# Tying weight sums and transposes behind products, and gating one conv quarter earlier, in a one-core hybrid decoder layer

## The chip, the cores and the metric

The kernel runs on one core of one Trainium2 chip. The time of a run is the device time of that core in microseconds (us); the lower the better. The kernel before was run three times: 2455.8, 2457.36 and 2458.04 us, median 2457.36. One more execution was taken with the hardware profiler on; every duration below comes from it.

The engines of the core are named as the profile names them: PE (TensorE, matrix products), PEld (its weight loads, which overlap the products), DVE (VectorE, elementwise), ACT (ScalarE, activations and copies), POOL (GpSimd, which here issues DMAs and does little else) and SP (SyncE, which issues the weight loads). Each engine takes its instructions in the order of its own queue and waits at the head of it.

## The reference

One layer, 512 tokens, model width 2048, float32 throughout. Cut to what matters here:

```python
h = rmsnorm(x, g_mix)
z = h @ w_in                                  # conv B, C, V | Q, K, V | forget logits | two gates
conv_y = cb * causal_dwconv(cc * cv, conv_w)
conv_branch = conv_y @ w_conv_out             # 1024 -> 2048
attn = forgetting_attention(q, k, v, log_f)
attn_branch = attn @ w_attn_out               # 1024 -> 2048
merged = sigmoid(gate_c + b_c) * conv_branch + sigmoid(gate_a + b_a) * attn_branch
x = x + merged @ w_mix_out                    # 2048 -> 2048
h = rmsnorm(x, g_mlp)
u = square(relu(h @ w_ff1))                   # 2048 -> 8192
x = x + u @ w_ff2
return rmsnorm(x, g_final)
```

## The kernel before

**Products.** Most of the large products are done as seven products of half-size blocks instead of eight (a Strassen-Winograd scheme). The names are those of the scheme: A11 and A12 first (a group's head), then S1, S3, S2, S4 and A22 (its tail; the last mix group takes S1, S2, S4, S3, A22). The moving or stationary activations have seven forms of the same names, made by sums of their four quarters; the weights X[i, j] are summed on DVE while the group runs. Every float32 operand is split into a high part (rounded to fp32r, ACT) and a low part (the rest, DVE), and each block is multiplied three times: high by high, high by low, low by high. `Group.run` (L207) does this for one product: `split` writes a tile th and a tile tl (two buffers each), PE multiplies, and then the hook `self.after[name]` is called, which is where other work is placed between products. One product of 256 columns is 48 matmuls in the mix and the MLP's first product, and 24 in the conv output product, whose contraction is half as long.

**A group's order.** `head` (L241) loads X[0,0] and X[1,0], runs A11 and A12 and puts the first quarter of the output (0,0). `tail2` (L305) loads X[0,1] and X[1,1]; its *first sum* is X[0,1] - X[0,0], which S1 needs, its *third sum* X[1,1] - X[0,1], which S3 needs. It puts (1,1) after S2, (0,1) after S4 and (1,0) after A22. `first_sum` (L298) is a form of the first sum that is called from a hook: it loads X[0,1], and pins the sum. A pin (`tc.keep_in_program_order`) tells the planner, which otherwise orders each engine's queue by its own model of when inputs are ready, that an instruction may not be placed ahead of the one written just before it on the same engine. It says nothing about what may come in between, and adds no wait. Once a group is pinned, its third sum is pinned as well. In the kernel before only mix group 0 calls `first_sum`.

**The stages around the change**, each in four column quarters c or groups g of 512 columns:

- conv output products (`conv_out`, L918), in the order conv_out(0), attn_out(0), conv_out(1), (2), (3). Quarter 0 is multiplied by its gate where it is made; the others are stored to the DRAM tile held_d without a gate and brought back later (`bring`).
- attention output products (`attn_out`, L966), (1), (2), (3). `cons_at` takes one of the four 128-row results j: for c > 0 it loads the conv gate (hg), multiplies the conv branch by it (`onto`, L941), loads the attention gate (gt), multiplies the result by that and adds. A quarter's finished branch is then split into the seven operand parts M (`Products`, L869; `quads`, L885). The parts of quarter 3 go to two tiles, t2 and t3, which held the attention's operands: t3 those of the first chunk of the contraction, t2 those of the second. The parts of quarters 0 to 2 are made earlier. Those of quarter 3 are made from within the last attention product (A11, A12) and from the hooks of mix group 0.
- mix groups 0 to 3 (`Mix`, L1043, and the loop at L1133). `Mix.put` adds the residual (a load xr) to an output quarter, sums its squares, stores it and appends its transposition to `waiting`. `turn_waiting` (L1119) empties that list at chosen hooks: four PE transposes (ptr, L1075) for a quarter, two ACT copies with the gain into the tiles F (L1084), and for the quarter (0,1) two stores f_d of F's first half. `Mix.sums` forms the next operand's sums in place in F, and `out` splits and stores them (h_d). In group 3 `begin_part` loads the stored parts back into tiles that the mix no longer reads, as the operands of the MLP, and `fourth` loads the residual of the quarter (1,0).
- the first MLP group g0 (L1232), whose hooks finish the parts of group 3.

The pool `main` has a ring of five buffers with the tag "o", which the evacuated outputs, hg, gt, xr and the operand sums share. POOL issues the loads and stores of all these intermediate tiles from one queue; SP issues the loads of the weights and gt.

Of the kernel before, what the change touches and what calls it, by code (L numbers as in the profile page):

```python
# [45 lines left out]
def tile_hybrid_block(ctx: ExitStack, tc, x, g_mix, w_in, b_f, b_gate, conv_w, w_conv_out,  # L46
# [137 lines left out]
    class Group:  # L184
# [3 lines left out]
        def __init__(self, view, c1, c2, w, ST, mm, banks, put, scale=1.0, extra={}, after={}, shift=SHIFT):  # L188
            self.extra, self.after, self.shift = extra, after, shift
            self.view, self.cs, self.w, self.ST, self.mm, self.banks = view, (c1, c2), w, ST, mm, banks  # L190
            self.put, self.scale, self.at = put, scale, {}
            self.pinned = False
            self.nq = view.shape[0] // (2 * P)
# [722 lines left out]
    merged, quads3 = {}, {}  # L916

    def conv_out(c, banks):  # L918

        gates = {}  # L920
        if c == 0:
            for i, j in ((0, 0), (1, 1), (0, 1), (1, 0)):
                gates[i, j] = pc_.tile([P, 2, HS], F32, tag="hg", name="gates", bufs=4)
                k = 4 * c + 2 * j
                nc.gpsimd.dma_start(out=gates[i, j],
                                    in_=g_d[0, k:k + 2, :, i * HS:(i + 1) * HS].rearrange("k p s -> p k s"))
            place_merged(c)

        def put(i, j, v):
            ts = slice(i * HS, (i + 1) * HS)  # L930
            if c == 0:
                nc.vector.tensor_tensor(out=whole_of[c][:, i, :, j, :], in0=v, in1=gates[i, j], op=ALU.mult)
            else:
                nc.gpsimd.dma_start(out=held_d[c, 2 * j:2 * j + 2, :, ts].rearrange("k p s -> p k s"), in_=v)

        whole(Columns(w_conv_out, c * S, c * S + HS, HS, YS.get, mm_cols, tuple((b,) for b in banks), put,
                      extra={"A11": "first", "S3": "first"}))
# [28 lines left out]
    def attn_out(c, banks, last=False, **how):  # L966

        def cons_at(j, ps):
            if c > 0:
                hg = otile([P, S], "hg")  # L970
                nc.gpsimd.dma_start(out=hg, in_=g_d[0, 4 * c + j])
                onto(c, j, hg, ALU.mult)
# [4 lines left out]
            if last and j == 2:  # L977
                M.place(2, [(n, 3) for n in ("A11", "A12", "S1", "S2")])
                M.place(3, [("S4", 3), ("S3", 3), ("A22", 3), ("A22", 2)])
                for e in range(2):  # L980
                    nc.gpsimd.dma_start(out=M.at["A22", 2][e].bitcast(F32), in_=m22[e].bitcast(F32))
                quads3.update(M.quads(3, merged[3]))
                quads3["A11"]()
# [59 lines left out]
    class Mix:  # L1043
# [25 lines left out]
        def turn(self, i, j, v):  # L1069
# [3 lines left out]
            for par in range(2):  # L1073
                for t in range(2):
                    nc.tensor.transpose(pt[:, par, t * P:(t + 1) * P], v[:, t, par * P:(par + 1) * P], ident)  # L1075
# [46 lines left out]

    class Steps(dict):
# [9 lines left out]
    for g in range(4):  # L1133
        mix = Mix(g)
        after = Steps()
        if g == 0:
            for n, n2 in zip(("A12", "S1", "S3", "S2", "S4"), ("S1", "S3", "S2", "S4", "A22")):
                after.add(n, quads3[n2])
        if g == 3:
            after.add("S1", lambda: begin_part("A12", 4))  # L1140
        for n in ("A11", "S1", "A22") if g < 3 else ("A11", "S1", "S3"):
            after.add(n, turn_waiting)
        if before:
# [5 lines left out]
        else:  # L1149
            after.add("A12", lambda: begin_part("A11", 0))  # L1150
            after.add("S2", lambda: begin_part("S1", 1), lambda: begin_part("S3", 2))
            after.add("S4", mix.fourth, lambda: split_part("A11"))
            after.add("S3", lambda: begin_part("S2", 5))
            after.add("A22", lambda: begin_part("S4", 6), lambda: begin_part("A22", 3), lambda: split_part("A12"))
# [78 lines left out]
    g0.after = Steps(A11=[turn_waiting, mix.sums], A12=[lambda: mix.out("S1", mix.parts["S1"]),  # L1233
# [251 lines left out]
```

## Time and profile before

| | us |
|---|---|
| median of three runs | 2457.36 |
| the runs | 2455.8 to 2458.04 |
| the profiled execution, its own time | 2464.36 |
| its span, first to last instruction | 2462.6 |
| PE idle in the span (2462.6 - 2408.8) | 53.8 |
| conv_out(2) and (3), mix groups 0 to 3 and the first two products of the MLP | about 924 to 1239, with the attention products at 967 to 1033 |

How to read the views: a row of instructions gives the source line, the engine, the operation, the tiles written and read, the shape and the count; in the view in order of time it begins with its start and its duration, and the bracket at its end is how long the engine was idle ahead of it and what ended that. In a view of groups, the numbers behind the bar are the busy time, the mean duration in ns and the idle time ahead of them. A row of waits gives who waited for whom, the total in us, how often, and the longest. L104 is the low part of every split, L103 the high part, L113 every subtraction and L116 every addition. Matmuls are pipelined, so each lasts longer than the distance to the next one.

### The profile page before, as it was taken

Reading aid. Unit: us, or ns where it says so; the run is one execution under the profiler, and the core shown is the slowest. Engines: PE = TensorE matmul, PEld = TensorE weight load, DVE = VectorE, ACT = ScalarE, POOL = GpSimd, SP = SyncE. Lnnn points to the kernel's source line nnn. Section 1 sums busy time; section 2 is a strip of 40 time slices with the busy share of each in tenths; the row PEclk is TensorE's granted clock in tenths of the full one; section 3 lists DMA queues with packets and bytes.
Section 4 is the critical chain, followed back from the end, with each engine's and each line's share of the span. In section 5 each row is a group of like instructions: output and inputs, shape, how many; then the busy total and the mean of one; then the engine's idle time right before and its main releaser. Section 6 shows DMA issues by size and latency. Waiting matters only on the chain.

```text
span 2462.6 us, 41554 instructions
## 1 busy us (share of the span) xinstructions
PE 2408.8 (98%) x17800; PEld 2264.8 (92%) x17800; DVE 2041.8 (83%) x1729; ACT 1201.8 (49%) x1233; POOL 279.8 (11%) x450
## 2 busy tenths in 40 slices
PE   8999999999999999899899999999999999999998
PEld 8999899999999998799899999999997888888886
DVE  7987777788887777878888898888988888889898
ACT  6433443445555534355566666656655333333334
POOL 0100000111111112112200000000011000100000
PEclk9999999999999999999999999999999999999999
DMA  7664544454655746647855646556487576655662
GB/s 249 186 191 145 157 130 136 137 180 153 206 186 194 246 154 216 205 127 232 289 196 204 236 171 225 208 204 231 174 302 270 178 256 216 244 183 184 249 221 104
DMA packets 286588, 490.92 MB, mean 199 GB/s; under 512 B 11884, under 2 KB 198372, under 8 KB 286020
## 3 DMA queue, kind: packets, MB, share of 16 engines
q1 hardware_dynamic: 236032, 282.15, 36.0%
q0 software_dynamic: 49504, 205.02, 22.4%
q8 instruction: 139, 2.28, 0.4%
q10 hardware_dynamic: 868, 1.10, 0.1%
q14 instruction: 45, 0.37, 0.0%
HBM read 377.60 MB, written 110.10 MB: 198 GB/s over the span
## 4 chain that ended last, share of the span: by engine, by line
PE 48%; DVE 4%; DMA 3%; issue 2%; ACT 1%; POOL 0%; DVEq 0%; POOLq 0%; ACTq 0%
PE a L175 5%; PE a L173 5%; PE a L172 5%; PE a L153 3%; PE a L155 3%; PE a L157 3%; PE d L175 2%; PE d L153 2%; PE d L155 2%; PE d L172 2%; PE d L173 2%; PE d L157 2%; DVE tl L104 2%; PE c L153 1%; PE c L155 1%
## 5 line engine op out<-in xcount | busy, mean ns | idle before, releaser
L104 DVE TENSOR_TENSOR tl<-x,th 128x2048 fp32r<-128x2048 f32 (+1 forms) x280 | 639.1, 2288 | 177.0 <-ACT th L103 162.0
L103 ACT ACTIVATE th<-x 128x2048 fp32r<-128x2048 f32 (+1 forms) x280 | 536.9, 1918 | 498.6 <-DVE x L113 161.3
L113 DVE TENSOR_TENSOR x<-x,x 128x2048 f32<-128x2048 f32 (+1 forms) x160 | 365.9, 2287 | 29.8 <-DMA x<-in_w_in_dram 16.0
L103 ACT ACTIVATE th<-y 128x2048 fp32r<-128x2048 f32 (+1 forms) x109 | 185.0, 1701 | 276.0 <-PE a L173 138.8
L104 DVE TENSOR_TENSOR tl<-y,th 128x2048 fp32r<-128x2048 f32 (+1 forms) x109 | 219.0, 2013 | 26.0 <-ACT th L103 25.5
L172 PE MATMUL a<-th,us 128*128 128x512 f32 x512 | 199.4, 389 | 1.8 <-ACT th L103 1.8
L173 PE MATMUL a<-th,us 128*128 128x512 f32 x512 | 199.2, 389 | 0.0
L153 PE MATMUL c<-S,th 128*128 128x256 f32 x848 | 196.5, 277 | 0.0
L155 PE MATMUL c<-S,th 128*128 128x256 f32 x848 | 196.0, 277 | 0.0
L153 PE MATMUL a<-S,th 128*128 128x256 f32 x784 | 182.2, 278 | 0.0
L155 PE MATMUL a<-S,th 128*128 128x256 f32 x784 | 180.8, 276 | 0.0
L153 PEld LDWEIGHTS c<-S,th 128*128 128x128 f32 x848 | 159.3, 188 | 0.3
L155 PEld LDWEIGHTS c<-S,th 128*128 128x128 f32 x848 | 159.3, 188 | 0.0
L155 PEld LDWEIGHTS a<-S,th 128*128 128x128 f32 x784 | 147.3, 188 | 0.0
L153 PEld LDWEIGHTS a<-S,th 128*128 128x128 f32 x784 | 147.2, 188 | 0.0
L175 PE MATMUL a<-tl,us 128*128 128x512 f32 x512 | 136.9, 389 | 0.6 <-DVE tl L104 0.6
L153 PE MATMUL b<-A,th 128*128 128x256 f32 x544 | 127.2, 278 | 0.0
L155 PE MATMUL b<-A,th 128*128 128x256 f32 x544 | 127.1, 278 | 0.0
L153 PE MATMUL d<-S,th 128*128 128x256 f32 x544 | 126.4, 278 | 0.0
L153 PE MATMUL a<-A,th 128*128 128x256 f32 x544 | 126.2, 277 | 0.0
L155 PE MATMUL a<-A,th 128*128 128x256 f32 x544 | 126.0, 277 | 0.0
L155 PE MATMUL d<-S,th 128*128 128x256 f32 x544 | 125.8, 277 | 0.0
(377 smaller groups left out, 6069.1 us busy)
## 6 DMA issues: line engine op xcount, KB each, us to landing
x<-in_w_in_dram SPq DMA_DIRECT2D x86, 1024.0 KB, 5.9
x<-in_w_ff_dram SPq DMA_DIRECT2D x64, 1024.0 KB, 8.3
y<-in_w_ff_dram SPq DMA_DIRECT2D x64, 1024.0 KB, 7.6
us<-s_d POOLq DMA_DIRECT2D x48, 1024.0 KB, 9.5
s_d<-rh POOLq DMA_DIRECT2D x32, 896.0 KB, 5.4
s_d<-r POOLq DMA_DIRECT2D x32, 896.0 KB, 6.3
x<-in_w_mix_out_dram SPq DMA_DIRECT2D x16, 1024.0 KB, 8.2
g_d<-o POOLq DMA_DIRECT2D x32, 256.0 KB, 3.0
```

The costliest lines, as they stand in the source:

```text
L103: a = nc.scalar.activation(out=hi, in_=src, func=AF.Copy, scale=one)
L104: b = nc.vector.tensor_tensor(out=lo, in0=src, in1=hi.bitcast(F32), op=ALU.subtract)
L113: return nc.vector.tensor_tensor(out=out, in0=a, in1=b, op=ALU.subtract)
L153: nc.tensor.matmul(o, hi[:, q, js], Sh, start=first and q == 0 and j == 0, stop=False, skip_group_check=True)
L155: nc.tensor.matmul(o, hi[:, q, js], Sl, start=False, stop=False, skip_group_check=True)
L157: nc.tensor.matmul(o, lo[:, q, js], Sh, start=False, stop=q == nq - 1, skip_group_check=True)
L172: nc.tensor.matmul(o, Sh, hi[:, q, :], start=begin and q == 0, stop=False, skip_group_check=True)
L173: nc.tensor.matmul(o, Sl, hi[:, q, :], start=False, stop=False, skip_group_check=True)
L175: nc.tensor.matmul(o, Sh, lo[:, q, :], start=False, stop=q == nq - 1, skip_group_check=True)
```

## The change

- `first_sum` is hooked behind A12 in all conv output groups and in the first MLP group, there after the split of the operand part S1.
- The transposes of the mix outputs are pinned behind the matmuls written before them. In groups 0 to 2 the hook behind A22 now turns only one quarter, (1,1), and (0,1) is turned with (1,0) behind the next group's A11. In group 3 the hook behind A22 also turns: (1,1) there, no longer in the MLP group.
- Conv quarter 3 is gated where it is made, like quarter 0, but in place and then stored; `attn_out(3)` neither loads hg nor multiplies by it.
- Tiles t2 and t3 change places for the parts of quarter 3, and so for the MLP parts S3 and A22 that take these tiles later. The copy of the staged part A22 of quarter 2 goes to t2 with it.
- The parts of quarter 3 that the hooks of mix group 0 make (S1, S3, S2, S4, A22) are each hooked one product earlier. S1's comes ahead of `first_sum` in the same hook, so the pinned sum is behind it.
- In group 3 the residual load `fourth` moves from behind S4 to behind S1.

```diff
-        def __init__(self, view, c1, c2, w, ST, mm, banks, put, scale=1.0, extra={}, after={}, shift=SHIFT):
-            self.extra, self.after, self.shift = extra, after, shift
+        def __init__(self, view, c1, c2, w, ST, mm, banks, put, scale=1.0, extra={}, after=None, shift=SHIFT):
+            self.extra, self.after, self.shift = extra, {} if after is None else after, shift
...
+    GATED = (0, 3)
...
-        if c == 0:
+        if c in GATED:
             for i, j in ((0, 0), (1, 1), (0, 1), (1, 0)):
                 gates[i, j] = pc_.tile([P, 2, HS], F32, tag="hg", name="gates", bufs=4)
...
+        if c == 0:
             place_merged(c)
...
             else:
+                if c in GATED:
+                    nc.vector.tensor_tensor(out=v, in0=v, in1=gates[i, j], op=ALU.mult)
                 nc.gpsimd.dma_start(out=held_d[c, 2 * j:2 * j + 2, :, ts].rearrange("k p s -> p k s"), in_=v)
 
-        whole(Columns(w_conv_out, c * S, c * S + HS, HS, YS.get, mm_cols, tuple((b,) for b in banks), put,
-                      extra={"A11": "first", "S3": "first"}))
+        group = Columns(w_conv_out, c * S, c * S + HS, HS, YS.get, mm_cols, tuple((b,) for b in banks), put,
+                        extra={"A11": "first", "S3": "first"})
+        group.after["A12"] = group.first_sum
+        whole(group)
...
-            if c > 0:
+            if c not in GATED:
                 hg = otile([P, S], "hg")
...
-                M.place(2, [(n, 3) for n in ("A11", "A12", "S1", "S2")])
-                M.place(3, [("S4", 3), ("S3", 3), ("A22", 3), ("A22", 2)])
+                M.place(3, [(n, 3) for n in ("A11", "A12", "S1", "S2")])
+                M.place(2, [("S4", 3), ("S3", 3), ("A22", 3), ("A22", 2)])
...
-                    nc.tensor.transpose(pt[:, par, t * P:(t + 1) * P], v[:, t, par * P:(par + 1) * P], ident)
+                    tc.keep_in_program_order(
+                        nc.tensor.transpose(pt[:, par, t * P:(t + 1) * P], v[:, t, par * P:(par + 1) * P], ident))
...
+    def turn_first():
+        waiting.pop(0)()
+
...
-            for n, n2 in zip(("A12", "S1", "S3", "S2", "S4"), ("S1", "S3", "S2", "S4", "A22")):
+            for n, n2 in zip(("A11", "A12", "S1", "S3", "S2"), ("S1", "S3", "S2", "S4", "A22")):
                 after.add(n, quads3[n2])
         if g == 3:
-            after.add("S1", lambda: begin_part("A12", 4))
-        for n in ("A11", "S1", "A22") if g < 3 else ("A11", "S1", "S3"):
+            after.add("S1", mix.fourth, lambda: begin_part("A12", 4))
+        for n in ("A11", "S1") if g < 3 else ("A11", "S1", "S3", "A22"):
             after.add(n, turn_waiting)
+        if g < 3:
+            after.add("A22", turn_first)
...
-            after.add("S2", lambda: begin_part("S1", 1), lambda: begin_part("S3", 2))
-            after.add("S4", mix.fourth, lambda: split_part("A11"))
+            after.add("S2", lambda: begin_part("S1", 1), lambda: begin_part("S3", 3))
+            after.add("S4", lambda: split_part("A11"))
             after.add("S3", lambda: begin_part("S2", 5))
-            after.add("A22", lambda: begin_part("S4", 6), lambda: begin_part("A22", 3), lambda: split_part("A12"))
+            after.add("A22", lambda: begin_part("S4", 6), lambda: begin_part("A22", 2), lambda: split_part("A12"))
...
-    g0.after = Steps(A11=[turn_waiting, mix.sums], A12=[lambda: mix.out("S1", mix.parts["S1"]),
+    g0.after = Steps(A11=[turn_waiting, mix.sums], A12=[lambda: mix.out("S1", mix.parts["S1"]), g0.first_sum,
                                                         lambda: factors(common, turned)])
```

## The prediction

> **What bounds the kernel now.** I read the page first, then the busy times stretch by stretch over the part of the program that the diff touches (conv_out(2) to the first products of the MLP), then what TensorE (PE) waited for there, then VectorE (DVE) in order of time at each of those places.
>
> ```profile
> span 2462.6 us, 41554 instructions
> PE 2408.8 (98%) x17800; PEld 2264.8 (92%) x17800; DVE 2041.8 (83%) x1729; ACT 1201.8 (49%) x1233; POOL 279.8 (11%) x450
> ```
>
> PE is the bound nearly everywhere, so only time in which it waits or runs slowly can be won. The next view gives each stretch its length, then busy time and instructions of PE, PE's weight loads, DVE, ACT and POOL, the granted clock, and the share and rate of the DMA engines.
>
> ```profile
> 927.00:966.00 39.00, 36.52 (x312) 35.56 (x312) 31.66 (x34) 19.41 (x24) 5.65 (x8) 1.00 0.43 136
> 1033.00:1058.00 25.00, 16.12 (x98) 15.13 (x97) 14.82 (x21) 6.62 (x7) 0.71 (x1) 0.73 0.20 65
> 1058.00:1090.00 32.00, 28.94 (x248) 28.11 (x247) 26.40 (x22) 16.20 (x22) 2.91 (x4) 1.00 0.56 165
> 1090.00:1131.00 41.00, 40.41 (x352) 40.18 (x350) 34.94 (x29) 24.15 (x41) 12.34 (x20) 1.00 0.71 225
> 1131.00:1175.00 44.00, 41.69 (x353) 41.50 (x352) 36.04 (x29) 24.30 (x41) 12.34 (x20) 0.96 0.65 214
> 1175.00:1206.00 31.00, 29.19 (x258) 28.99 (x257) 29.60 (x25) 20.28 (x35) 9.84 (x16) 1.00 0.62 205
> 1206.00:1221.00 15.00, 12.70 (x110) 12.53 (x110) 11.35 (x13) 11.17 (x19) 4.30 (x7) 1.00 1.06 386
> 1221.00:1239.00 18.00, 13.40 (x104) 13.16 (x103) 13.44 (x13) 7.74 (x15) 5.76 (x8) 0.91 1.02 391
> 1239.00:1277.00 38.00, 38.00 (x337) 38.00 (x337) 33.46 (x30) 21.95 (x23) 2.13 (x3) 1.00 0.41 136
> ```
>
> The last stretch has no wait: 38.00/337 = 0.1128 us per matmul of 256 columns. Length minus count times 0.1128 is what each other stretch loses, slow matmuls included: 3.8 (conv_out 2 and 3), 14.0 and 4.0 (mix group 0), 1.3 and 4.2 (groups 1 and 2), 1.9 and 2.6 (group 3), 6.3 (first products of the MLP). Sum 38.1 us; no more than that is to be had here. PE's waits in the stretch name the culprits:
>
> ```profile
> PE ptr L1075 <- DVE o L116: 11.6, 5, 4.6
> PE a L172 <- ACT M L103: 5.7, 1, 5.7
> PE a L173 <- DVE M L104: 1.9, 1, 1.9
> PE b L157 <- DVE tl L104: 1.9, 2, 1.2
> ```
>
> Transposes (ptr) wait for rows of the residual, the first mix product for its last operand parts M, two conv products for the low half of a weight.
>
> **Conv: the first sum, and the gate.** At both conv waits DVE stands behind a weight sum whose load has not landed, with the low half of A12 behind it:
>
> ```profile
> 927.55 1.23 DVE L113 TENSOR_TENSOR y<-y,y 128x1024 f32<-128x1024 f32 x1 [3.49 <-DMA y<-in_w_conv_out_dram]
> 928.69 0.68 DVE L116 TENSOR_TENSOR o<-d,o 128x512 f32<-128x512 f32 x1
> 929.29 1.21 DVE L104 TENSOR_TENSOR tl<-y,th 128x1024 fp32r<-128x1024 f32 x1
> L103 ACT ACTIVATE th<-x 128x2048 fp32r<-128x2048 f32 x32 | 61.2, 1913 | 42.6 <-PE a L173 16.8 <-DVE x L113 14.1 <-PE d L173 7.5
> ```
>
> The change ties the sum behind A12's low half, and the third sum behind S1's. The load's place on SP's queue stays. The sum then starts at 927.55 as now, but nothing needed earlier is behind it; it ends at 928.8, the high half of its split (half of the 1.9 of 2048 columns, an estimate of 1.0) at 929.8. A12's low half was there at 930.5 and its last eight matmuls took 0.9, so A12 ended at 931.4, without the wait of 1.2 at 930.2, and S1 is due then. So all 3.8 would return. The gate puts four 128x512 operations of 0.68 (2.7 us) into conv_out(3), whose DVE is 81% busy; its gaps, 7.3 us over two conv quarters, cover it on average; uncovered it costs 2.7. Its four loads pass from late in POOL's queue to conv_out(3), where the DMA engines are 43% busy. I take 3.0, bounds 1.0 and 3.8.
>
> **Mix group 0.** In the last attention product DVE stood still for the gate's load, then had to multiply by it (the last two rows are the issues of the attention gates in that stretch and their time to landing):
>
> ```profile
> L948 DVE TENSOR_TENSOR merged<-merged,hg 128x256 f32<-128x256 f32 x16 | 6.3, 420 | 10.1 <-DMA hg<-g_d 10.0
> 1040.00 0.42 DVE L948 TENSOR_TENSOR merged<-merged,hg 128x256 f32<-128x256 f32 x1 [3.72 <-DMA hg<-g_d]
> 1046.21 1.89 DVE L104 TENSOR_TENSOR M<-merged,M 128x512 fp32r<-128x512 f32 x3
> L104 DVE TENSOR_TENSOR tl<-x,th 128x2048 fp32r<-128x2048 f32 x31 | 70.9, 2287 | 24.4 <-ACT th L103 24.4
> L974 SPq DMA_DIRECT2D gt<-g_d x2: 339/478/618, 1028.7 to 1030.0; - x2
> DMA to landing us min/median/max: 10.6/11.0/11.5
> ```
>
> Eight of the 16 small multiplications (3.4 us), their four loads and the wait go. With tiles 2 and 3 exchanged, the parts A11, A12, S1 and S2 of quarter 3 go where the attention's first four operand blocks lay, which is read out one chunk earlier, so A11's part can be ready before the last attention matmul. S1's part moves ahead of the first sum, which is tied behind it, and both go behind A11. A12's part: gate 0.68, two additions of 0.42, a split of 0.7 on ACT and 0.7 on DVE after the last attention matmul, 2.9 us, against A11's 48 matmuls of 5.4 us. It is covered if the gate loads landed. Then DVE sets the pace: from there to A22's low half it has six splits of 2.29, four weight sums of 2.29, some ten operations of 0.68 on the parts, the two last gated evacuations (3.0) and seven operations of 0.68 on the outputs: 37.5 us against 7x48x0.1128 = 37.9 for PE. So near a tie leaves waits; of 18.0 I return 15 and leave 3. Bounds: all 18.0, and 9 (the waits of 5.7 and 1.9 for M, and little of the slow clock). The copies of m22 now wait on POOL for the end of the last attention product, with residual rows behind them, due some 11 us later.
>
> The 14.0 is 25.00 - 16.12 = 8.9 us of idle PE and 5.1 us of slow matmuls: 0.73 of the clock was granted in that stretch. [...]
>
> **The transposes.** Behind groups 0 to 2 PE turns (1,1), does eight matmuls of the next A11, then waits for (0,1) (the last row is of the six stores f_d):
>
> ```profile
> 1131.00 0.60 PE L1075 MATMUL ptr<-ident,o 128*128 128x128 f32 x4
> 1134.84 0.92 PE L1075 MATMUL ptr<-ident,o 128*128 128x128 f32 x4 [2.31 <-DVE o L116]
> 1131.89 2.29 DVE L113 TENSOR_TENSOR x<-x,x 128x2048 f32<-128x2048 f32 x1 [2.17 <-DMA x<-in_w_mix_out_dram]
> 1134.10 0.68 DVE L116 TENSOR_TENSOR o<-o,xr 128x512 f32<-128x512 f32 x1
> 1137.50 0.68 DVE L116 TENSOR_TENSOR o<-o,xr 128x512 f32<-128x512 f32 x1
> 1146.46 0.69 DVE L113 TENSOR_TENSOR f<-s,f 128x512 f32<-128x512 f32 x1
> L1084 ACT ACTIVATE f<-ptr,cols 128x256 f32<-128x256 f32 x32 | 13.4, 463 | 5.3 <-DVE M L104 2.5 <-DMA h_d<-f 2.1 <-PE ptr L1075 0.4
> DMA to landing us min/median/max: 3.6/3.8/4.3
> ```
>
> Tied and moved behind A11, the transposes of (0,1) come at 1131.0 + 0.5 + 5.4 = 1136.9, and their rows are ready at 1134.8: no wait. Those of (1,0) follow at 1137.4 and their rows at 1138.2: 0.8 stays, in three groups 2.4. Of 1.3 + 4.2 + 1.9 = 7.4 I return 5.0. The store f_d of the first half, issued behind (0,1), now goes one product later, and the subtraction that overwrites its source (1146.46) must wait for it: 1136.9 + 0.5 + two copies of 0.46 + two issues (about 1.1) and 3.8 is 1143.2, about when the subtraction would come without PE's wait. Bounds 0 and 7.4.
>
> In group 3 (0,1) was behind S3 already. Its rows are late because DVE splits A11's part first, and DVE is 95% busy in 1175:1206. Nothing there is taken away: 0 of 2.6, bounds 0 and 2.6.
>
> **Group 3 into the MLP.**
>
> ```profile
> 1222.75 2.29 DVE L113 TENSOR_TENSOR x<-x,x 128x2048 f32<-128x2048 f32 x1 [4.49 <-DMA x<-in_w_ff_dram]
> 1224.96 0.68 DVE L116 TENSOR_TENSOR o<-d,o 128x512 f32<-128x512 f32 x1
> 1228.22 2.29 DVE L113 TENSOR_TENSOR x<-x,x 128x2048 f32<-128x2048 f32 x1 [2.57 <-DMA x<-in_w_ff_dram]
> 1230.43 0.68 DVE L116 TENSOR_TENSOR o<-o,xr 128x512 f32<-128x512 f32 x1
> 1231.17 1.11 PE L1075 MATMUL ptr<-ident,o 128*128 128x128 f32 x4 [4.60 <-DVE o L116]
> L1054 POOL DMA_DIRECT2D xr<-in_x_dram x1: 719/719/719, 1209.6 to 1209.6; - x1
> DMA to landing us min/median/max: 12.4/12.4/12.4
> ```
>
> Two sums wait for loads ahead of the last rows (1,0), and PE, there at 1231.17 - 4.60 = 1226.6, stands 4.6 us. Tied, both sums stand behind; the rows are then ready by about 1225, if their residual has landed: it took 12.4 us from 1209.6 (the last two rows), to 1222.0. The change issues it two products earlier, behind S1, past POOL's part loads and stores.
>
> New is the path to S1: two copies (0.93), the addition (0.69), the split of its operand (0.7 and 0.7), only now the first sum (2.29), then its high half (1.91): 7.2 us against 49 matmuls of A12, 5.5. 1.7 us appear at S1, and the third sum, now also late, costs some 1.2 at S3. Return 3.4 of 6.3; bounds -2 (both sums and the other operand splits in line first, about 5 more) and 6.3.
>
> **Sum.** 3.0 + 15 + 5.0 + 0 + 3.4 = 26.4 us, against the profiled execution's 2464.36 (span 2462.6): 2438. It lies 7.0 above the median 2457.36, so for the runs 2457.4 - 26.4 = **2431 us**. Bounds together: -38.1 (2419) to -8.0 (2449).
>
> **Rivals.** *DVE becomes the bound (0.22).* For: group 3 has 29.60 + 11.35 = 41.0 us of DVE work for 368 PE instructions, 41.5 us; group 0 is the tie above. Against: DVE now idles behind PE's own waits. Then group 0 returns 9, groups 1 to 3 only 3, the MLP 2, conv 2: 16, 2441.
>
> *The attention gate's loads take the wait's place (0.08).* The last two gt loads sat in the same crowd of transfers as hg; if they land 11 us after the last issues near 1030, A12's part waits 4 us, with half clock about 7. Against: hg takes its buffers from the same ring of five (tag o), and four of these tiles go. 2457.4 - 19 = 2438.
>
> *The ties do not bind (0.08).* They forbid only earlier places; if other stalls of the same size fill in (the third-product sums, the tight M parts), less than 4 returns: 2455.
>
> *Slower: the f_d store (0.07).* If it lands as late as the residual row (12.4 instead of 3.8), DVE stands 8.6 us in three groups, 26 us, eating the whole return, and each such wait slows the matmuls behind it, by 5.1 us in 1033:1058 and 6.3 - 4.6 = 1.7 in 1221:1239, say 3 each: 2457.4 - 26.4 + 26 + 9 = 2466. It decides from a landing of about 10 us on. Against: the six stores landed within 3.6 to 4.3.
>
> **Numbers.** Forecast 0.55, own range 2421 to 2438. The measurement tells 0.2% (4.9 us) from no change. Faster: 0.55 + 0.22 + 0.08 and little else, 0.84; same 0.08; slower 0.08. Range 2421 to 2448, leaving out the last two rivals and the extreme bounds.
>
> **What would show it.** In the changed profile: no DVE wait for y loads ahead of a low half; PE's waits for M gone and clock 1.00 behind the attention; transposes waiting under 1 us, except some 2.5 in group 3; a new wait of 1 to 2 us at the MLP's S1 for its weight's high half. It would be wrong if the tied sums or the f_d store show DVE waits above 5 us, or if mix group 0 still takes over 48 us.

## The result, and the profile after

The change leaves the time as it was: 2455.74 us (median of 12 runs, 2451.32 to 2460.74) against 2457.02 for the kernel before on the same chip (12 runs, 2453.5 to 2463.0), a ratio of 0.9997 with a 95% interval of 0.9986 to 1.0008. Of 26.4 us that were forecast, at most some 3 are there. The profiled execution after took 2454.27, with this span and these busy times on the page:

```profile
span 2452.6 us, 41546 instructions
PE 2408.9 (98%) x17800; PEld 2263.6 (92%) x17800; DVE 2043.4 (83%) x1725; ACT 1202.0 (49%) x1233; POOL 279.7 (11%) x450
```

PE's idle time is 2452.6 - 2408.9 = 43.7 us, where it was 53.8. The stretches after, in the view of busy times, columns as before. The first row has the borders of the prediction's first row (conv_out(2) and (3) now run from 928.6 to 970.7); the others are two parts of mix group 0, parted at S3's first matmul, groups 1, 2 and 3, and the MLP's first products:

```profile
927.00:966.00 39.00, 36.84 (x315) 36.06 (x315) 32.40 (x34) 18.10 (x22) 5.08 (x7) 1.00 0.42 141
1037.92:1060.73 22.81, 18.71 (x149) 17.48 (x147) 20.79 (x27) 11.18 (x16) 3.96 (x6) 1.00 0.20 68
1060.73:1085.40 24.67, 24.64 (x195) 24.45 (x196) 19.95 (x12) 11.65 (x14) 0.73 (x1) 0.93 0.64 185
1085.40:1127.00 41.60, 41.03 (x353) 40.43 (x352) 35.65 (x30) 24.05 (x41) 12.33 (x20) 1.00 0.69 227
1127.00:1168.00 41.00, 41.00 (x356) 40.70 (x355) 35.70 (x30) 24.42 (x41) 12.30 (x20) 1.00 0.71 227
1168.00:1210.00 42.00, 40.64 (x356) 40.16 (x354) 38.54 (x35) 27.35 (x50) 13.43 (x22) 1.00 0.79 272
1210.00:1225.00 15.00, 12.69 (x110) 12.41 (x108) 12.17 (x14) 10.82 (x18) 6.66 (x9) 1.00 0.99 377
1225.00:1242.00 17.00, 14.28 (x109) 13.89 (x110) 14.91 (x13) 7.58 (x8) 0.01 (x1) 0.90 0.53 199
```

By the prediction's measure (length less matmuls times 0.1128 us) the first row loses 3.5 us, where 3.8 were lost: nothing came back in conv. Group 0 loses 22.81 - 16.81 = 6.0 in its first part and 24.67 - 22.00 = 2.7 in the rest, 8.7 where 3 were to be left. Groups 1, 2 and 3 lose 1.8, 0.8 and 1.8, the last two rows 2.6 and 4.7. What PE waited for from conv_out(0) to the MLP's first group, the six largest (in us in total, times, longest):

```profile
PE a L153 <- ACT th L103: 4.8, 5, 1.3
PE c L153 <- ACT th L103: 2.4, 1, 2.4
PE d L172 <- ACT th L103: 2.1, 1, 2.1
PE ptr L1082 <- DVE o L116: 1.4, 1, 1.4
PE pt L401 <- DVE tl L104: 1.3, 1, 1.3
PE d L146 <- ACT th L103: 1.1, 2, 0.9
```

Of the 5.7 and 1.9 us for M 0.7 are left, of the 11.6 for the transposes 2.0. The largest waits are now for **th**, the high half of a weight sum, in conv and the MLP (L153) and in the mix (L172): the very sums that the change tied, and those behind them.

One profile is one execution, so I measured the stretches in the traces of all runs below, from the first matmul of a stage to the first of the next. These lengths in us are worked out from the traces' matmuls (the expectations below add rounded group lengths and can differ by 0.1):

```
                        before, its repeat   after, two repeats     order of before     order of after
conv_out(0)               19.3, 19.3         21.7, 21.9, 21.3       19.3                21.6
conv_out(1)               19.3, 19.3         20.9, 20.9, 20.9       19.3                20.9
conv_out(2)               21.0, 21.2         20.6, 22.1, 21.9       21.0                21.6
conv_out(3)               21.4, 21.4         21.4, 21.6, 21.4       21.2                21.5
conv_out(0) to (3)        80.9, 81.1         84.6, 86.6, 85.5       80.8 (8 traces)     85.5 (5 traces)
last attention product    22.2, 22.3         23.3, 23.7, 23.2       22.7 (5)            23.3 (9)
mix group 0               57.1, 55.5         47.5, 47.5, 47.0       55.6 (5)            47.1 (9)
mix groups 1 to 3        130.6, 132.4       124.8, 123.1, 125.6    129.6 (8)           125.4 (5)
  from there to MLP S2    29.3, 23.4         30.4, 30.7, 30.2       24.8 (8)            30.2 (5)
mix group 1 to MLP S2    159.9, 155.7       155.2, 153.8, 155.7    154.4 (8)           155.7 (5)
```

The last two columns are means over all kernels with the one or the other order in that stretch, whatever they do elsewhere. Their differences are +4.7 in conv, +0.6 in the last attention product (no more than single traces of one order differ), -8.5 in group 0 and +1.3 from group 1 to the MLP's S2: -1.9 together, which agrees with the -0.7 of the ratio (0.0003 of 2457; interval -3.4 to +2.0). So mix group 0 did pay and conv took half of it back. Groups 1 to 3 became 4.2 us shorter, and the MLP's entrance behind them 5.5 us longer. In conv, 3.9 of the 4.7 us lie in quarters 0 and 1.

### The profile page after: what moved, and what is told of

It is laid out like the page before. It is cut to its first block, busy times and chain, and to the rows that moved or that the text cites. A ratio compares the mean times of both kernels' runs of the same rounds, so it can differ in the third digit from the quotient of the medians.

```text
span 2452.6 us, 41546 instructions
## 1 busy us (share of the span) xinstructions
PE 2408.9 (98%) x17800; PEld 2263.6 (92%) x17800; DVE 2043.4 (83%) x1725; ACT 1202.0 (49%) x1233; POOL 279.7 (11%) x450
## 3 DMA queue, kind: packets, MB, share of 16 engines
q8 instruction: 139, 2.28, 0.4%
## 4 chain that ended last, share of the span: by engine, by line
PE 47%; DVE 4%; issue 3%; DMA 2%; ACT 1%; POOL 0%; DVEq 0%; POOLq 0%; ACTq 0%
PE a L175 4%; PE a L173 4%; PE a L172 4%; PE a L153 3%; PE a L157 3%; PE a L155 3%; PE d L175 2%; PE d L173 2%; PE d L172 2%; PE d L155 2%; PE d L153 2%; PE d L157 2%; DVE tl L104 2%; PE c L155 1%; PE c L157 1%
## 5 line engine op out<-in xcount | busy, mean ns | idle before, releaser
L172 PE MATMUL a<-th,us 128*128 128x512 f32 x512 | 199.4, 389 | 1.0 <-ACT th L103 1.0
L153 PE MATMUL c<-S,th 128*128 128x256 f32 x848 | 197.8, 278 | 2.4 <-ACT th L103 2.4
L153 PE MATMUL a<-S,th 128*128 128x256 f32 x784 | 182.3, 278 | 1.1 <-ACT th L103 1.1
L153 PEld LDWEIGHTS c<-S,th 128*128 128x128 f32 x848 | 160.3, 189 | 2.8 <-ACT th L103 2.5
L153 PEld LDWEIGHTS a<-S,th 128*128 128x128 f32 x784 | 147.2, 188 | 1.3 <-ACT th L103 1.3
L153 PE MATMUL b<-A,th 128*128 128x256 f32 x544 | 126.4, 277 | 0.0
L153 PE MATMUL d<-S,th 128*128 128x256 f32 x544 | 126.3, 278 | 0.0
L153 PE MATMUL a<-A,th 128*128 128x256 f32 x544 | 126.0, 277 | 0.0
```

What stands on the lines that cost most here:

```text
L153: nc.tensor.matmul(o, hi[:, q, js], Sh, start=first and q == 0 and j == 0, stop=False, skip_group_check=True)
L172: nc.tensor.matmul(o, Sh, hi[:, q, :], start=begin and q == 0, stop=False, skip_group_check=True)
```

## The experiments

All ratios are to the kernel before on the same chip, with the 95% interval. They are not the quotients of the medians and differ from them by up to 0.0013.

**The two kernels again, in one profiled execution each** (before_again, after_again). No edit.

> The kernel before, profiled once more. The profiled execution that the prediction used was 7 us above the median of the runs, the one of the changed kernel 1 us below its own. Theory (the profile of before was an unlucky execution): mix group 0, 57 us from its first matmul to the transposes behind it, comes out at 50 us or less, and the losses of conv_out(2) to the MLP's second product sum to about 31 us instead of 38. Rival (its losses are typical): 56 to 58 us and 37 to 39 us again, and the missing gain has to lie in the changed kernel.

> The changed kernel, profiled once more. Its first profile shows waits for ACT's high halves in the conv output groups (S2's first matmul, 0.6 to 1.3 us in each) and at S1, S3 and S2 of the first MLP group (2.4, 0.9, 1.1 us). Theory (they come from the new order of DVE's queue): the same waits at the same places within 0.5 us. Rival (chance of the transfers): other places or none.

Measured: before 2462.11 in that execution, with the kernel before at a median of 2460.76 there (21 runs); after 2456.07. Each theory came half true. In the repeat of before mix group 0 took 55.5 us and not 50, so its losses are typical, as the rival had it; but from conv_out(2) to the MLP's S1, without the attention products, it is 5.8 us shorter, 4.4 of them behind group 0. In the repeat of after the waits in conv are there again (3.9 us in all where the first profile had 3.7), and so is the one at the MLP's S1 (2.4). But S3 waited 2.0 us where it had waited 0.9, and S2 not at all where it had waited 1.1.

What matters is in PE's waits of the two executions of the kernel before. The prediction rests on a wait of 4.60 us at 1231.17; in the repeat, from 1080 on, all waits of the transposes together are these:

```profile
PE ptr L1075 <- DVE o L116: 7.4, 4, 3.1
```

instead of 11.6 in five. The MLP's entrance, from the end of group 3's last matmul to S1, took 12.0 us and not 18.2, while group 3 took 48.4 and not 45.1. The 4.6 us were one execution's share of a wait that moves about between group 3 and the entrance.

**The third sum let go** (third_free), in the changed kernel:

```diff
-            if self.pinned:
+            if self.pinned and self.mm is mm_rows:
                 tc.keep_in_program_order(third)
```

> The changed kernel, but the third weight sum of the conv output groups is not tied (DVE takes it ahead of S1's low half again, as before the change). Theory (tying the third sum behind S1's low half put first sum, S1's split, third sum, S3's split, the next sum and S2's split into one chain): the waits at S2's first matmul in the four conv groups go, some 4 us, time 2452, ratio to before about 0.998. Rival (the gate's multiplications and the operand splits of the attention fill DVE): the waits stay, 2455 to 2456.

The flag also frees the third sum of the MLP's first group, but there DVE takes it in the same place as in the changed kernel, behind S1's low half. Measured: 2453.54, ratio 0.9976 [0.9967, 0.9985]; conv 79.9 us. First the changed kernel at conv_out(2), in order of time: DVE, ACT, PE.

```profile
930.77 1.23 DVE L113 TENSOR_TENSOR y<-y,y 128x1024 f32<-128x1024 f32 x1
933.21 1.23 DVE L104 TENSOR_TENSOR tl<-y,th 128x1024 fp32r<-128x1024 f32 x1 [1.21 <-ACT th L103]
934.35 1.22 DVE L113 TENSOR_TENSOR y<-y 128x1024 f32<-128x1024 f32 x1
936.77 1.22 DVE L104 TENSOR_TENSOR tl<-y,th 128x1024 fp32r<-128x1024 f32 x1 [0.61 <-ACT th L103]
938.03 2.48 DVE L113 TENSOR_TENSOR y<-y,y 128x1024 f32<-128x1024 f32 x2
...
935.68 1.06 ACT L103 ACTIVATE th<-y 128x1024 fp32r<-128x1024 f32 x1 [2.03 <-DVE y L113]
939.37 2.02 ACT L103 ACTIVATE th<-y 128x1024 fp32r<-128x1024 f32 x2 [2.63 <-DVE y L113]
...
940.48 0.38 PE L153 MATMUL a<-ys,th 128*128 128x256 f32 x1 [0.58 <-ACT th L103]
```

The first sum (930.77) is followed by idle DVE until ACT has S1's high half, then by S1's low half (933.21), and only then comes the third sum (934.35), because it is tied behind that low half. Its own halves follow (935.68, 936.77), then the next two sums, S2's among them (938.03), whose high halves on ACT (939.37) end after PE has arrived (940.48). With the third sum free, the same place reads:

```profile
929.75 1.23 DVE L113 TENSOR_TENSOR y<-y,y 128x1024 f32<-128x1024 f32 x1 [0.47 <-DMA y<-in_w_conv_out_dram]
931.69 1.23 DVE L113 TENSOR_TENSOR y<-y 128x1024 f32<-128x1024 f32 x1 [0.72 <-DMA y<-in_w_conv_out_dram]
932.83 1.22 DVE L104 TENSOR_TENSOR tl<-y,th 128x1024 fp32r<-128x1024 f32 x1
934.57 1.22 DVE L104 TENSOR_TENSOR tl<-y,th 128x1024 fp32r<-128x1024 f32 x1
935.82 2.48 DVE L113 TENSOR_TENSOR y<-y,y 128x1024 f32<-128x1024 f32 x2
```

The third sum fills the time in which ACT rounds the first, and the next two sums start 935.82 - 929.75 = 6.1 us after the first one instead of 938.03 - 930.77 = 7.3. Over all conv groups and the first attention products PE then waited for these two things alone, 0.8 us:

```profile
PE c L153 <- DVE o L116: 0.4, 1, 0.4
PE a L153 <- ACT th L103: 0.4, 1, 0.4
```

**The conv ties alone** (conv_only), in the kernel before (with `after=None`, as in the change):

```diff
-        whole(Columns(w_conv_out, c * S, c * S + HS, HS, YS.get, mm_cols, tuple((b,) for b in banks), put,
-                      extra={"A11": "first", "S3": "first"}))
+        group = Columns(w_conv_out, c * S, c * S + HS, HS, YS.get, mm_cols, tuple((b,) for b in banks), put,
+                        extra={"A11": "first", "S3": "first"})
+        group.after["A12"] = group.first_sum
+        whole(group)
```

> The kernel before with the first sums (and with them the third) of the conv output groups tied, nothing else. Theory (the tie of the third sum costs more than the tie of the first returns): the four conv groups take 84 to 85 us against 81.0 and 81.2 before and 84.6 to 86.5 in the changed kernel; ratio 1.001 to 1.002. Rival (it is the gate's multiplications): 81 us or less, ratio 0.999 to 1.000.

Measured: 2461.29, ratio 1.001 [0.9999, 1.0021]; conv 85.5 us against 80.8. Together with the run before it this shows the step: the tie of the third sum costs some 5.6 us (85.5 to 79.9, three traces with it free), the tie of the first alone returns 0.9 (80.8 to 79.9). That 0.9 is 2.0 returned in quarters 2 and 3, where the waits were, and 1.1 lost in quarters 0 and 1, which had hardly any.

**The gating and the earlier parts alone** (parts_only; again as parts_again, beside the changed kernel as after_beside), in the kernel before:

```diff
+    GATED = (0, 3)
-        if c == 0:
+        if c in GATED:
...
+                if c in GATED:
+                    nc.vector.tensor_tensor(out=v, in0=v, in1=gates[i, j], op=ALU.mult)
...
-            if c > 0:
+            if c not in GATED:
...
-                M.place(2, [(n, 3) for n in ("A11", "A12", "S1", "S2")])
-                M.place(3, [("S4", 3), ("S3", 3), ("A22", 3), ("A22", 2)])
+                M.place(3, [(n, 3) for n in ("A11", "A12", "S1", "S2")])
+                M.place(2, [("S4", 3), ("S3", 3), ("A22", 3), ("A22", 2)])
...
-            for n, n2 in zip(("A12", "S1", "S3", "S2", "S4"), ("S1", "S3", "S2", "S4", "A22")):
+            for n, n2 in zip(("A11", "A12", "S1", "S3", "S2"), ("S1", "S3", "S2", "S4", "A22")):
```

with the tiles of `begin_part` for S3 and A22 exchanged as in the change.

> The kernel before with conv quarter 3 gated where it is made, the exchanged tiles and the operand parts one product ahead, nothing tied anew. Theory (these carry the return of mix group 0; DVE, busy without a pause from 1034 to 1072 in the changed kernel, sets what is left): mix group 0 at 47 to 48 us against 55.5 to 57.1, att3 one us longer as in the changed kernel, conv as before; ratio about 0.997. Rival (group 0 needs the tied transposes too): 51 us or more.

> parts_only again, beside the others on one chip: ratio to before 0.995 to 0.997 (10.3 us less was measured: 2447 to 2449 where before takes 2457).

> The changed kernel again, beside parts_again on one chip: if its other parts cost what they did one by one (turns +2.9, conv +2.5 us over before), it lies 4 to 10 us above parts_again and at a ratio of 0.998 to 1.000; if the loss is chance of the chip, within 2 us of parts_again.

Measured: 2449.7, ratio 0.9958 [0.9944, 0.9973]; on another chip again 2448.97, ratio 0.9962 [0.9947, 0.9977], beside the changed kernel with 2457.01, ratio 1.0 [0.9991, 1.0008]. This part alone is worth 9 to 10 us by the ratios, 7.7 and 8.4 by the medians, and the changed kernel lies 8.0 above it on the same chip: the rest of the change costs what this part brings. Group 0 takes 47.0 and 46.9 us here as in the changed kernel, and conv_out(3), where the four gate multiplications went, takes 21.5 and 21.1, against 21.4 and 21.4 in the two traces of before. The gate's multiplications cost nothing that shows.

**What holds group 0 at 47 us.** In the changed kernel S3's wait for its weight, in order of time (DVE, ACT, PE):

```profile
1047.06 2.28 DVE L113 TENSOR_TENSOR x<-x,x 128x2048 f32<-128x2048 f32 x1
...
1056.40 2.28 DVE L113 TENSOR_TENSOR x<-x,x 128x2048 f32<-128x2048 f32 x1
1058.77 1.91 ACT L103 ACTIVATE th<-x 128x2048 fp32r<-128x2048 f32 x1 [1.21 <-DVE x L113]
1060.73 0.39 PE L172 MATMUL d<-th,M 128*128 128x256 f32 x1 [2.12 <-ACT th L103]
```

Neither sum has a bracket: DVE came to them straight from other work, and from the group's first matmul to 1060.73 it was busy 20.79 of 22.81 us. To test whether DVE's load is the bound, I took the parts' low halves off it, in the kernel with this part alone. Once on ACT (lows_on_act), as a copy that puts the whole part where its rest belongs:

```diff
             def put(n, src):
-                split(src, *self.at[n, c])
+                hi, lo = self.at[n, c]
+                if c < 3:
+                    split(src, hi, lo)
+                else:
+                    for o in (hi, lo):
+                        nc.scalar.activation(out=o, in_=src, func=AF.Copy, scale=1.0)
```

and once on GpSimd (lows_on_pool), as the subtraction that it is:

```diff
+                    nc.scalar.activation(out=hi, in_=src, func=AF.Copy, scale=1.0)
+                    nc.gpsimd.tensor_tensor(out=lo, in0=src, in1=hi.bitcast(F32), op=ALU.subtract)
```

> parts_only, with the low halves of the last conv quarter's seven operand parts filled by a copy on ScalarE instead of a subtraction on VectorE: they hold the whole part and not its rest, so the values differ, the matmuls do not. Theory (VectorE sets the pace of mix group 0): five subtractions of 0.68 us (3.4 us) leave VectorE there, and group 0 falls from 47.0 us to 43 to 44.5 and the time by 2.5 to 4 us. Rival (the pace is set by loads or by ScalarE's high halves): group 0 stays at 46.5 to 48, the time within 1 us of parts_again or above.

> parts_only, with the seven low halves of the last conv quarter's operand parts subtracted on GpSimd instead of VectorE; the values are the reference's. Theory (VectorE sets the pace of mix group 0, as lows_on_act showed with 41.0 us for 47.0): VectorE is rid of the same work, group 0 takes 42 to 45 us and the time falls to 2443 to 2447, ratio 0.994 to 0.996. Rival (a subtraction on GpSimd is so long that the parts come late, or it slows VectorE's own operations): group 0 at 47 or more and no gain on parts_again.

Measured with the copies on ACT: 2443.63, ratio 0.9938 [0.9924, 0.9951], group 0 at 41.0 us. The theory held, with more than it forecast. Not five but all seven subtractions lie behind the group's first matmul in the trace of after, 4.8 us of DVE. PE's waits in the group fell from 5.0 us in the second profile of the gating and parts (parts_again) to a single one of 0.7; the longest of each:

```profile
PE d L172 <- ACT th L103: 2.2, 1, 2.2
PE b L175 <- DVE tl L104: 0.7, 1, 0.7
```

The copy also has no need of the high half, so the parts can be ready sooner; but PE had waited only 0.7 of the 5.0 us for parts, the rest for weights and their halves. Why the remaining 1.7 of the 6.0 us went, in matmuls that run closer together, no run shows. Group 0 then runs from 1032.9 to 1073.9; a window of the same length, 2 us later, reads

```profile
1035.00:1076.00 41.00, 39.62 (x342) 39.22 (x343) 35.93 (x29) 27.12 (x38) 3.48 (x6) 1.00 0.50 146
```

where 342 matmuls at 0.1128 are 38.6 us. With the subtractions on GpSimd: 2450.69, ratio 0.9963 [0.995, 0.9976], group 0 at 48.0: nothing gained, the rival's result. Six of GpSimd's seven subtractions, between 1030 and 1062 us (busy us, mean ns, idle ahead; the seventh has another source and took 3.33 us), and, in order of time, two of DVE's own operations beside them:

```profile
L895 POOL TENSOR_TENSOR M<-merged,M 128x512 fp32r<-128x512 f32 x6 | 12.8, 2140 | 28.6 <-ACT M L894 28.6
```

```profile
1039.44 3.39 DVE L113 TENSOR_TENSOR x<-x,x 128x2048 f32<-128x2048 f32 x1
1042.75 3.35 DVE L104 TENSOR_TENSOR tl<-x,th 128x2048 fp32r<-128x2048 f32 x1
```

2.14 us in the mean, 1.27 at the least, for what takes 0.68 on DVE, and DVE's 2.28 and 2.29 became 3.39 and 3.35. These two lie beside GpSimd's subtractions between 1039.21 and 1047.25. DVE's next operation of this size (1047.72) took 2.28, with a GpSimd subtraction of 2.60 beginning 0.83 us after it. By what means DVE's operations lengthen, and what a GpSimd subtraction takes while DVE is idle, no run shows.

**The transposes alone** (turns_only), in the kernel before:

```diff
-                    nc.tensor.transpose(pt[:, par, t * P:(t + 1) * P], v[:, t, par * P:(par + 1) * P], ident)
+                    tc.keep_in_program_order(
+                        nc.tensor.transpose(pt[:, par, t * P:(t + 1) * P], v[:, t, par * P:(par + 1) * P], ident))
...
-        for n in ("A11", "S1", "A22") if g < 3 else ("A11", "S1", "S3"):
+        for n in ("A11", "S1") if g < 3 else ("A11", "S1", "S3", "A22"):
             after.add(n, turn_waiting)
+        if g < 3:
+            after.add("A22", turn_first)
```

> The kernel before with the transposes alone changed (tied, (0,1) turned behind the next A11, (1,1) behind A22 in group 3). Its profile's stage lengths: mix groups 1 to 3, 130.6 and 132.4 us in two profiles of before, 124.8 and 123.1 in two of the changed kernel. Theory (this part carries the return of groups 1 to 3, as the prediction had it): 123 to 126 us there, mix group 0 unchanged at 55 to 57, time ratio about 0.997. Rival (that return comes from group 0 being on time, DVE with it): 129 us or more, ratio 0.999 to 1.001.

Measured: 2461.16, ratio 1.0012 [1.0002, 1.0021]: a little slower. Groups 1 to 3 took 124.9 us against 129.6 in the mean of the eight traces with the order of before, so the waits between the groups did go, and nearly all that was forecast came back there. The expected gain in time did not come, because the MLP's entrance took it back (DVE, ACT, PE in order of time):

```profile
1216.27 0.48 DVE L1082 SCALAR_TENSOR_TENSOR A<-ptr,cols,A 128x256 fp32r<-128x256 f32 x1
1222.91 2.29 DVE L113 TENSOR_TENSOR x<-x,x 128x2048 f32<-128x2048 f32 x1 [6.16 <-DMA x<-in_w_ff_dram]
1225.12 0.48 DVE L1082 SCALAR_TENSOR_TENSOR A<-ptr,cols,A 128x256 fp32r<-128x256 f32 x1
1225.63 0.84 ACT L1085 ACTIVATE f<-ptr,cols 128x256 f32<-128x256 f32 x2 [5.30 <-DVE A L1082]
1226.52 1.12 PE L1076 MATMUL ptr<-ident,o 128*128 128x128 f32 x4 [5.48 <-ACT f L1085]
```

The MLP's first sum, not tied in this kernel, stood 6.16 us for its load. Behind it on DVE stood the low half of an operand (1225.12), behind that ACT's copies out of the transposed quarter (0,1) (1225.63), and these free the PSUM bank that (1,1) shares in group 3 (bank 6): 5.48 us of PE at one place.

**The MLP's first sum**, taken out of the changed kernel (mlp_free), and, the other way round, added to the transposes in the kernel before (turns_mlp):

```diff
-    g0.after = Steps(A11=[turn_waiting, mix.sums], A12=[lambda: mix.out("S1", mix.parts["S1"]), g0.first_sum,
+    g0.after = Steps(A11=[turn_waiting, mix.sums], A12=[lambda: mix.out("S1", mix.parts["S1"]),
```

> The changed kernel without the tie of the first MLP group's first sum (its first and third sum float ahead, as before the change). Theory (tied behind the operand split S1, the sum makes S1 of the MLP wait, then S3 and S2): the three waits of 2.4, 0.9 and 1.1 us go and a wait of the transposes behind the MLP's A11 for the rows (1,0) comes back, up to 4.6 us with slow matmuls: 2454 to 2458. Rival (the waits come from the rest of DVE's work there): the three waits stay and the transposes wait as well, 2458 to 2461.

> Before, with the transposes and the MLP's first sum of the change (its two sums tied behind the second product's operand), and neither the gating nor the conv ties. Theory (these two belong together and return nothing: mix groups 1 to 3 up to the MLP's third product are held to 153 to 157 us by VectorE and loads, whatever the order): that stretch takes 153 to 157.5 us, the long wait for the transposes that turns_only had at the MLP's entrance (5.5 us) is gone, and the time lies within 3 us of before (ratio 0.999 to 1.001). Rival (the pair is worth the 5.0 + 3.4 us that the prediction gave it): ratio 0.9965 to 0.998, the stretch under 151 us.

Measured: without it 2459.15, ratio 0.9997 [0.9988, 1.0006], on the rival's side of 2458. But the three waits did go, and the wait of turns_only is there again (3.6 us, for the same copies and not for the rows (1,0)). With transposes and first sum in the kernel before: 2462.0, ratio 1.0008 [0.9997, 1.0019], and 156.5 us from group 1 to the MLP's S2 against 154.4, as expected. The pair removes the waits at its two places and is worth nothing. The long wait is only replaced by this, in the changed kernel (DVE, then PE):

```profile
1218.34 0.69 DVE L116 TENSOR_TENSOR s<-f 128x512 f32<-128x512 f32 x1 [1.50 <-ACT f L1091]
1221.41 2.29 DVE L113 TENSOR_TENSOR x<-x,x 128x2048 f32<-128x2048 f32 x1
...
1225.70 0.58 PE L153 MATMUL c<-S,th 128*128 128x256 f32 x1 [2.44 <-ACT th L103]
1233.67 0.35 PE L146 MATMUL d<-S,th 128*128 128x192 f32 x1 [0.92 <-ACT th L103]
```

The sum now starts behind five operations on the operand's sums and halves (1218.34 to 1221.41), and S1 and S3 wait for its high half and the next. S2 waits another 1.1 us at 1240.61.

**Versions put together.** One (best) is the changed kernel with the third sum free as above, in conv and the MLP, and the MLP's first sum one place earlier:

```diff
-    g0.after = Steps(A11=[turn_waiting, mix.sums], A12=[lambda: mix.out("S1", mix.parts["S1"]), g0.first_sum,
+    g0.after = Steps(A11=[turn_waiting, mix.sums], A12=[g0.first_sum, lambda: mix.out("S1", mix.parts["S1"]),
```

the other (parts_conv) the gating and parts with the conv ties, third sum free.

> The changed kernel with the third sums tied in the mix group alone, and the first MLP group's first sum tied ahead of the operand split S1 instead of behind it. Theory (each tied sum lengthens the chain of whatever it is placed behind): conv groups about 79.8 us as with the free third sum, the wait at the MLP's S1 under 1 us, S1 to S2 of the MLP 11.5 us instead of 14.9; time ratio 0.996. Rival (DVE is full there in any order): S1 to S2 stays at 14 to 15 us, ratio 0.9976 as with the free third sum alone.

> Before, with the gating and earlier parts (as parts_only) and the conv products' first sums tied behind the second product's operand, their third sums left free; neither the transposes nor the MLP's first sum are touched. Theory (the tie of the third sum is what lost time in conv, the tie of the first is worth about 1.2 us): the four conv groups take 79.5 to 80.0 us together against 80.7 in parts_only, the time is 0.6 to 1.6 us under parts_again, the ratio to before 0.995 to 0.996. Rival (a conv group's length only follows where its loads land): conv 80.5 to 82 and no gain on parts_again.

Measured: 2449.14, ratio 0.9954 [0.9941, 0.9966], and 2450.57, ratio 0.9965 [0.9953, 0.9976]. Both beat the kernel before, the second also the changed kernel beside it (2457.01), and neither can be told from the gating and parts alone (2449.7 on the chip of the first, 2448.97 on that of the second). In the first conv took 79.8 us as expected, but S1 to S2 of the MLP took 14.1 us and not 11.5, the rival's result there: S1 now waits 1.5 us for its low half. In the second conv took 80.1 us against 80.9, and the expected gain in time did not come: its median is 1.6 us higher, and a difference of 1 us is under what these runs resolve.

## Why the prediction was wrong

It forecast 2431 and faster; the time is 2455.74, the same. By its own steps, with the term that it returned and the one found:

**Conv, 3.0: -4.7.** The step that failed is "the sum then starts at 927.55 as now, but nothing needed earlier is behind it". It looked at what stands behind the first sum and passed over the other half of its own argument, that the third sum goes behind S1's low half. Tied so, sum, high half and low half of S1, third sum and S3's halves follow one another on two engines, and S2's weight comes late in each group; third_free and conv_only show it. And the term was worked out for quarters 2 and 3 alone, while the change ties all four: quarters 0 and 1, which it put at nothing, lost 2.3 and 1.6 us of the 4.7. The bounds (1.0 to 3.8) excluded a loss without a reason. That the gate's multiplications hide in DVE's gaps was right.

**Mix group 0, 15: 8.5, less 0.6 in the attention product ahead of it.** The mechanism was right: M's waits and hg's went, and this is the main return of the change. The size is off. The step "So near a tie leaves waits" set DVE's work, 37.5 us, against PE's 37.9 over the whole group and left 3 us. The work is not spread so: up to S3 DVE is busy for 20.79 us and PE has 149 matmuls, 16.8 us, and 6.0 of the 8.7 us lost are there; lows_on_act took seven subtractions away and won 6 us. The rival that gave this term 9, DVE as the bound, had this term right, though not its total of 2441. The test named for it, that group 0 must not take over 48 us, was too loose: 47.5 passed it with 8.7 lost.

**The transposes, 5.0: 4.2. Group 3 into the MLP, 3.4: -5.5.** The waits between the groups went, and groups 1 to 3 returned about what was forecast. It did not reach the end. At the MLP's entrance the new waits at S1, S3 and S2 came, 2.44, 0.92 and 1.1 where 1.7, 1.2 and none were forecast, with the clock at 0.67 behind the first. Two steps failed. First, "the rows are then ready by about 1225" and the return of 3.4 were taken from a wait of 4.6 us that the repeat of the same kernel doesn't have at that place: from group 3's end to S2 the kernel before took 29.3 us in the profile at hand, 23.4 in its repeat and 24.8 in the mean of eight traces, so there was little to return. Second, the terms were added as if each wait removed shortened the end. From group 1 to the MLP's S2 the length stayed within 152 to 157 us in the fifteen other traces, whichever of these waits was there; the rows above show DVE busy 35.65 to 38.54 us of each 41 to 42 and the DMA engines at 0.99 in 1210:1225. That these two hold the length is argued from the rows; no run took the loads away, and none moved the load `fourth` by itself.

**The median.** The sum was subtracted from a median that lay 7.0 us under the profiled execution, though its terms were read off that execution. The prediction gave both numbers and didn't ask which of its losses made up the 7.0.

**The f_d store and the gt loads**, the rivals of 2466 and 2438, did not occur: in the trace of after DVE stood once, for 1.4 us, for an f_d store, whose six landed within 2.3 to 4.5 us, and once, for 0.7, for a gt load, whose last four landed within 2.9. The half clock that the rival of 2438 reckons with is in the profile before: the granted clock was 0.50 from 1041 to 1053, behind the wait of 5.69 us for M that ended at 1041.52. That a wait of 4 us would become 7 with it is the author's estimate; the wait did not come, and no run shows the 3 us. "The ties do not bind" gave 2455, the right time by luck, from another cause: the ties do bind, and that is what cost.

In sum: 7.7 us of the miss are conv, 7.1 group 0 with the attention product, 9.7 the transposes and the MLP, 24.5 of 26.4.

## What to carry to other kernels

When an instruction is tied in order, list everything that the same flag ties, and follow each to the engine that would have used the gap: a tie behind an operation that waits for another engine leaves that wait empty (1.21 us of DVE at 933.21). Work the term out for every place that the change touches, not only for those that have a wait to win. Weigh an engine's work against PE's product by product and not over a stage, since a stage that balances on the whole can be bound in its first half (DVE was busy for 20.79 of 22.81 us up to S3). And before a wait in one profile is counted as a gain, take a second profile of the same kernel: a return that belongs to one execution, or that the next wait on a loaded engine takes over, is none.

## What the runs showed of the hardware

Behind the same wait at the same place the granted clock fell in most executions and not in all. Nine traces have the wait for S3's weight in mix group 0: three of the changed kernel, and third_free, mlp_free, parts_only, parts_again, parts_conv and best. It is 2.12 to 2.27 us long in each. Over the 4.3 us behind it the granted clock was 0.60 to 0.67 in seven of them and 1.00 in two. The first two rows are busy times of the changed kernel behind its waits of 2.12 us (1060.73) and 2.44 us (1225.70); then comes the changed kernel in its third profile (after_beside), first the wait for S3's weight, 2.25 us, and then the busy times around and behind it. The granted clock is the third number from the end.

```profile
1060.70:1065.00 4.30, 4.27 (x23) 4.27 (x24) 4.25 (x2) 0.71 (x2) 0.00 (x0) 0.60 0.05 21
1225.70:1230.00 4.30, 4.30 (x26) 4.30 (x27) 4.30 (x7) 1.60 (x3) 0.00 (x0) 0.67 1.01 417
```

```profile
1061.58 0.38 PE L172 MATMUL d<-th,M 128*128 128x256 f32 x1 [2.25 <-ACT th L103]
```

```profile
1061.50:1065.80 4.30, 4.00 (x32) 3.80 (x33) 4.21 (x2) 0.76 (x3) 0.00 (x0) 1.00 0.13 48
```

So the granted clock fell behind waits of 2.1 to 2.4 us here, and not every time. In the kernel before it was 0.57 from 1135 to 1139, behind the wait of 2.31 us that ended at 1134.84. In 4.3 us the lower clock of the changed kernel cost 9 matmuls of 32, 1.0 us at 0.1128; from S3's first matmul to S2's the seven traces took 7.16 to 7.27 us and the two 6.60, so 0.6 us was left of it. The other thing not expected is the 2.14 us of a GpSimd subtraction and the 1.1 us that DVE's own operations lost beside it, above.
